# Attention's output blocks prepared in two parts and three kept on chip, and the Fourier gate columns moved from the projections into attention

## The chip, the cores and the metric

The kernel runs on one core of a Trainium2 chip. A core has TensorE (PE: matmuls; its weight loads are shown as PEld), VectorE (DVE), ScalarE (ACT), GpSimdE (POOL), and SyncE (SP), which here only issues DMA transfers. Each engine works through its own list of instructions in order, and they wait for one another through semaphores. The metric is the device time of one execution in microseconds. Less is better.

## The reference

Two layers over a latent stream of 1024 tokens and a context of 256, model width 1024. In each layer the rows are normalized and modulated (`shift` and `scale` from `c @ w_ada`), one projection to 2560 columns is split among three head groups, and one output projection joins them:

```python
px = split_cols(hx @ w_in[l])            # q 512, k 128, v 128, g_att 512, a 256, b 256, g_conv 256, f_u 256, g_four 256
attn   = windowed_attention(rope(q), rope(k), v, kc, vc, sink)  # 8 heads, 2 kv heads, 128-token blocks,
                                                                # keys: block-1, block, block+1, and all 256 of the context
y_conv = silu(layer_norm(depthwise_conv31(a * sigmoid(b))))
y_four = real(fft2(f_u)) @ w_four + b_four
y = concat([attn * silu(g_att), y_conv * silu(g_conv), y_four * silu(g_four)], -1)
x = x + gate * (y @ w_out[l])
```

The context stream goes through layer 0 in the same way (its attention is over its own keys alone); in layer 1 only its keys and values are needed. At the end comes one more normalization of the latent rows. All inputs are fp32.

## The kernel before

Every large product is made of three matmuls (`mm3`, lines 195 to 197): each operand is kept as a high part, rounded by ScalarE, and a low part, the rest, by a subtraction on Vector or GpSimd (`split`). Tokens lie in ten blocks of 128, 0 to 7 latent, 8 and 9 context. Projections go by 128 columns and chunks of 512, 512 and 256 tokens (`CHUNKS`; the context's chunk is left out in layer 1 but for keys and values). One chunk is 24 matmuls.

A layer has two stages:

**Projections.** `todo` lists the columns, `projections` makes them chunk by chunk: convolution input (`C_A`, `C_B`), then two tiles of Fourier gate columns (`C_GF`), keys, values, queries. After each chunk the loop takes one piece of side work from `side()`: the Fourier branch (`four`), the rope tables, the adaptive sums of this layer's gate (`gate_sums`) and, in layer 0, of the next layer's modulation (`ada1`: a piece with the sums of four loaded weight tiles, which starts the next four loads, then a piece that makes columns of them). It also takes convolution taps from the queue `back` (`fill_v`): 31 taps for each of two channel tiles and each token span, each one Vector instruction, up to a budget of time per chunk. The helper `Behind` puts these background instructions behind the last foreground instruction of Vector written before them.

**Attention.** `Attention.step` is one step of a software pipeline over (block, pair of heads), four to a block: scores of step i, transposes of the probabilities of step i-1, values and output of step i-2. Layer 0 has 40 steps of 10 blocks, layer 1 has 32 of 8, and each has two more that empty the pipeline. The latent blocks 1 to 6 have five key tiles of 128, 0 and 7 have four, the context blocks two. With each step goes one filler, a piece of other matmul work: first, from `rest()`, the rest of `pj` (attention gate columns `C_GATT`), with pieces of the convolution's norm `cn` once `back` is empty, then the convolution gate chunks (`C_GC`), and then the output projection in halves of 512 columns, `OP.half(i, h)`, which need block i's attention. `post` and `late` are queues of Vector work that wait for the next step's start or this step's end. Banks of the tags `mm` and `pt` (two each) hold matmul results in PSUM; fillers in attention use `mm` alone; `mmx` takes both by turns. `t512` is a small tile with four buffers.

The attention output of a block, `ot`, is stored to DRAM (`od`), and `Out.load` loads it back in the order of channels, with the other two branches' part (`yd`) and the attention gate (`sgd`). `Out.prep` gates the attention part and splits all 1024 columns, the low part on GpSimd while attention runs. In the loop, the halves of the last two blocks are left until after it.

The order of instructions on each engine is fixed when the program is built: a scheduler takes, at each simulated time, the ready instruction with the lowest priority number, and numbers rise in the order in which the code is written.

Of the kernel before, what the change touches and what calls it, by code (L numbers as in the profile page):

```python
# [16 lines left out]
ALU = mybir.AluOpType  # L17
# [4 lines left out]
P = 128  # L22
# [117 lines left out]
def tile_backbone(ctx: ExitStack, tc: tile.TileContext, a, out):  # L140
# [32 lines left out]
    def fill_v(us):  # L173
        V.background = True
        while back and us > 0:
            t, f = back.popleft()
            f()
            us -= t
        V.background = False

# [364 lines left out]
    def conv_taps(l, ct, u, z, spans):  # L545

        w = lambda j: cw[:, ct, l * KC + j:l * KC + j + 1]

        def first(s0, s1):
            V.tensor_scalar(out=z.cols(s0, s1), in0=u.cols(s0, s1), scalar1=w(15),  # L550
                            scalar2=col("conv_b", l * 2 + ct), op0=ALU.mult, op1=ALU.add)

        def tap(s0, s1, j):
            d = j - 15
            o0, o1 = max(s0, s0 - d), min(s1, s1 - d)
            V.scalar_tensor_tensor(out=z.cols(o0, o1), in0=u.cols(o0 + d, o1 + d), scalar=w(j),
                                   in1=z.cols(o0, o1), op0=ALU.mult, op1=ALU.add)
        for s0, s1 in spans:
            us = 1.25 if s0 == 0 else 0.4
            back.append((us, lambda a=(s0, s1): first(*a)))  # L560
            for j in range(KC):
                if j != 15:
                    back.append((us, lambda a=(s0, s1, j): tap(*a)))
        back.append((0.0, u.put))
# [276 lines left out]
    class Attention:  # L841
# [3 lines left out]
        def __init__(self, l, order, qd, kk, vv, od):  # L845
            self.l, self.qd, self.kk, self.vv, self.od = l, qd, kk, vv, od
            self.steps = [(b, pr) for b in order for pr in range(4)]
            self.q, self.st, self.done, self.next = {}, {}, [], 0
# [122 lines left out]
        def output(self, i):  # L971
            (b, pr), z = self.steps[i], self.st.pop(i)
            z["tmp"] = t512()[:, :256]
            r0, r1 = (slice(0, HD), slice(HD, P)) if pr < 2 else (slice(HD, P), slice(0, HD))
            S.activation(z["tmp"][r0], z["o"][r1], AF.Copy)
            ot = self.os[:, 0:512].rearrange("p (j t) -> p j t", j=4)
            r0 = slice(0, HD) if pr < 2 else slice(HD, P)
            j0 = (pr % 2) * 2
            V.tensor_tensor(out=ot[r0, j0:j0 + 2, :], in0=z["tmp"][r0].rearrange("p (h q) -> p h q", h=2),
                            in1=z["o"][r0].rearrange("p (h q) -> p h q", h=2), op=ALU.add)  # L980
            if pr == 3:
                nc.sync.dma_start(out=self.od[:, b * P:(b + 1) * P].rearrange("(j p) t -> p j t", p=P), in_=ot)
                self.os.put()
                self.done.append(b)
# [86 lines left out]
    class Out:  # L1071


        def __init__(self, l, order, wo, od, sgd, yd, x1d, xnd):
            self.l, self.order, self.wo, self.src = l, order, wo, (od, sgd, yd)
            self.x1d, self.xnd = x1d, xnd
            self.raw, self.y = {}, {}
# [3 lines left out]
        def load(self, i):  # L1081
# [6 lines left out]
            nc.sync.dma_start(out=yv[:, 0:4, :], in_=od[:, t0:t0 + P].rearrange("(k p) t -> p k t", p=P))  # L1088
# [6 lines left out]

        def prep(self, i):

            if i >= len(self.order) or i in self.y:
                return
            self.load(i)  # L1100
            (raw, yh, yl), yv, sg = self.raw[i]
            V.scalar_tensor_tensor(out=yv[:, 0:4, :], in0=yv[:, 0:4, :], scalar=0.5, in1=sg,
                                   op0=ALU.mult, op1=ALU.mult)
            split(yh, yl, raw)
            self.y[i] = yh, yl

        def half(self, i, h, bank, quick=False):
# [14 lines left out]
            for k in range(NK):  # L1122
                ks = slice(k * P, (k + 1) * P)
                mm3(o, (yh[:, ks], yl[:, ks]), (self.wo.hi[k][:, hs], self.wo.lo[k][:, hs]), k == 0, k == NK - 1)
# [156 lines left out]
    for l in range(DEPTH):  # L1281
# [39 lines left out]
        def side():  # L1321

            yield from four
            tab.extend(bufs.get("rope") for _ in range(2))
            for i, name in enumerate(("k_cos", "k_sin")):
                nc.sync.dma_start(out=tab[i].lat, in_=a[name])
# [43 lines left out]
        def gf_evac(m):  # L1370
            def f(o, c0, c1):
                drain(four)
# [27 lines left out]
        att = Attention(l, order, qd, kk, vv, od)  # L1400
# [3 lines left out]
        for m in range(2):  # L1404
            todo.append((C_GF + m * P, full) + gf_evac(m) + (mmx,))
# [6 lines left out]
        budget = [(3.0 if t[0] < C_V else 5.0) * (0.5 if c == 2 else 1.0) for t in todo for c in t[1]]  # L1412
# [4 lines left out]
        for i in range(q_at):  # L1417
            c = next(pj)
            steps(sd)
            if i >= k_at:  # L1420
                steps(kp)
# [14 lines left out]
        OP = Out(l, order, wo, od, sgd, yd, x1d, xnd)  # L1436
# [5 lines left out]
        def rest():  # L1442
# [3 lines left out]
            for i, c in enumerate(pj):  # L1446
                if i == 4 * len(full) - 2:
                    raw = w_begin(l, C_GC)
                if i == 4 * len(full) - 1:
# [46 lines left out]
        seq = deque([(0, 1), (1, 1)] + [(i, h) for i in range(2, end - 1) for h in range(2)])  # L1496
# [9 lines left out]
        while att.next < len(att.steps) + 2:  # L1506
# [5 lines left out]
            if loaded < end and loaded < len(att.done) and len(whole_ones) >= loaded - 1:  # L1512
                OP.load(loaded)
                loaded += 1
            can = seq and seq[0][0] in OP.y
            if loaded - 1 not in OP.y:
                late.append(lambda i=loaded - 1: OP.prep(i))
            att.step((lambda: next_half(mm)) if can else None)
        holding[0] = False
# [132 lines left out]
```

## Time and profile before

| | |
|---|---|
| median of 3 runs | 1202.81 us (1198.1 to 1203.62) |
| profiled execution | 1202.68 us, span of its instructions 1200.6 us |
| busy: PE, PEld | 1103.3 us (92%), 925.9 us (77%) |
| busy: DVE, ACT, POOL | 820.6 us (68%), 554.7 us (46%), 295.0 us (25%) |
| mean granted TensorE clock | 0.964 |
| DMA | 146.49 MB, mean 122 GB/s |

The span runs from the first to the last instruction of the profiled execution; what lies around it is the difference to that execution's time. The granted clock is a mean of two levels, 1.00 (2.4 GHz) and 0.50 (1.2 GHz). A matmul's end is modelled in the profile, so that successive ones overlap in it.

### The profile page before, as it was taken

What the parts mean: (1) busy time and instruction counts of PE and PEld (TensorE: products, weight loads), DVE (VectorE), ACT (ScalarE), POOL (GpSimd) and SP (SyncE); (2) the same over time, 40 slices, a digit from 0 to 9 for tenths busy, and PEclk for the clock granted to TensorE, in tenths of its full rate; (3) what the DMA queues carried; (4) which work ended last, traced back from release to release, by engine and by line L of the source; (5) the groups of instructions that cost most, each with busy time, mean ns of one, the idle gap of its engine ahead of it and who ended that gap; (6) DMA issues with size and microseconds to landing.
All of it is one profiled execution on the core that took longest, in us unless ns stands there. A gap on an engine that the chain in (4) does not pass through costs nothing.

```text
span 1200.6 us, 17131 instructions
## 1 busy us (share of the span) xinstructions
PE 1103.3 (92%) x6165; PEld 925.9 (77%) x6165; DVE 820.6 (68%) x1665; ACT 554.7 (46%) x1209; POOL 295.0 (25%) x266
## 2 busy tenths in 40 slices
PE   5799999999999989999889999999989979988866
PEld 3488887888888878888668788788778868877754
DVE  3425879999577786666755369889656786766654
ACT  5563222312566655564646652222255654545541
POOL 1212000000222443544342120000022453334321
PEclk9799999999999999999979999999989989999889
DMA  9602273744332433544436423532243453322221
GB/s 332 218 25 71 70 239 113 225 137 108 84 97 75 149 115 102 166 142 132 115 120 227 145 65 116 184 110 79 88 93 106 136 145 103 110 74 71 71 71 53
DMA packets 154093, 146.49 MB, mean 122 GB/s; under 512 B 7398, under 2 KB 131734, under 8 KB 154008
## 3 DMA queue, kind: packets, MB, share of 16 engines
q1 hardware_dynamic: 154008, 145.40, 39.5%
q8 instruction: 49, 0.80, 0.3%
q14 instruction: 36, 0.29, 0.1%
HBM read 110.49 MB, written 34.87 MB: 121 GB/s over the span
## 4 chain that ended last, share of the span: by engine, by line
PE 70%; DVE 10%; DMA 9%; ACT 4%; issue 3%; SPq 2%; POOL 1%; DVEq 0%; ACTq 0%; POOLq 0%
PE mm L195 13%; PE mm L197 13%; PE mm L196 13%; PE pt L195 5%; PE pt L196 5%; PE pt L197 5%; PE mm L963 4%; PE pt L949 4%; DMA od<-ot 3%; PE score L893 2%; DVE score L57 2%; DVE pl L57 2%; PE score L895 2%; DMA wr<-od 1%; ACT p L919 1%
## 5 line engine op out<-in xcount | busy, mean ns | idle before, releaser
L195 PE MATMUL mm<-hxh,wh 128*128 128x512 f32 (+1 forms) x808 | 311.5, 386 | 5.5 <-DVE t L57 3.2
L197 PE MATMUL mm<-hxh,wl 128*128 128x512 f32 (+1 forms) x808 | 306.7, 380 | 2.4 <-POOL wl L405 2.3
L196 PE MATMUL mm<-hxl,wh 128*128 128x512 f32 (+1 forms) x808 | 307.4, 380 | 0.0
L195 PEld LDWEIGHTS mm<-hxh,wh 128*128 128x128 f32 x808 | 153.8, 190 | 37.5 <-DVE t L57 4.3
L57 DVE SCALAR_TENSOR_TENSOR cy<-cu,cw,cy 128x1014 f32<-128x1014 f32 (+20 forms) x180 | 180.1, 1007 | 2.6
L197 PEld LDWEIGHTS mm<-hxh,wl 128*128 128x128 f32 x808 | 153.6, 190 | 30.3 <-POOL wl L405 3.1
L935 POOL TENSOR_SCALAR p<-p,st 128x640 f32<-128x640 f32 (+2 forms) x144 | 114.4, 809 | 249.1 <-DVE st L57 129.1
L196 PEld LDWEIGHTS mm<-hxl,wh 128*128 128x128 f32 x808 | 154.0, 191 | 25.0 <-issue 0.5
L405 POOL TENSOR_TENSOR wl<-wr,wh 128x1024 fp32r<-128x1024 f32 x26 | 64.2, 2468 | 396.3 <-ACT wh L404 394.1
L954 ACT ACTIVATE ph<-pt 128x512 fp32r<-128x512 f32 x184 | 97.4, 542 | 121.0 <-PE pt L949 118.2
L57 DVE TENSOR_TENSOR pl<-pt,ph 128x512 fp32r<-128x512 f32 x184 | 112.3, 616 | 57.8 <-ACT ph L954 56.4
L949 PE MATMUL pt<-ident,p 128*128 128x128 f32 x640 | 107.6, 286 | 24.5 <-DVE pl L57 19.1
L919 ACT ACTIVATE p<-score,st 128x640 f32<-128x640 f32 (+2 forms) x144 | 105.3, 734 | 36.5 <-DVE st L57 29.2
L57 DVE CUSTOM_DVE_ANT_0 score<-score,mask,nsink 128x640 f32<-128x640 f32 (+2 forms) x144 | 110.8, 782 | 13.8 <-PE score L895 13.0
L195 PE MATMUL pt<-hxh,wh 128*128 128x512 f32 (+1 forms) x296 | 112.2, 383 | 3.9 <-ACT hxh L393 2.5
L404 ACT ACTIVATE wh<-wr 128x1024 fp32r<-128x1024 f32 x56 | 59.7, 1066 | 116.5 <-PE mm L196 73.1
L196 PE MATMUL pt<-hxl,wh 128*128 128x512 f32 (+1 forms) x296 | 111.1, 376 | 0.7 <-DVE hxl L57 0.7
L197 PE MATMUL pt<-hxh,wl 128*128 128x512 f32 (+1 forms) x296 | 110.4, 373 | 0.9 <-DVE wl L57 0.9
L949 PEld LDWEIGHTS pt<-ident,p 128*128 128x128 f32 x640 | 79.8, 146 | 38.2 <-POOL p L935 8.7
L963 PE MATMUL mm<-ph,v 128*128 128x256 f32 x320 | 93.1, 314 | 13.2 <-ACT ph L954 10.7
L963 PE MATMUL mm<-pl,v 128*128 128x256 f32 x320 | 93.7, 315 | 5.3 <-DVE pl L57 4.9
L963 PEld LDWEIGHTS mm<-ph,v 128*128 128x128 f32 x320 | 64.6, 202 | 18.3 <-ACT ph L954 15.8
(220 smaller groups left out, 1797.8 us busy)
## 6 DMA issues: line engine op xcount, KB each, us to landing
wada<-w_ada SPq DMA_DIRECT2D x48, 512.0 KB, 7.0
wr<-w_in SPq DMA_DIRECT2D x38, 512.0 KB, 4.1
qq<-qd SPq DMA_DIRECT2D x36, 256.0 KB, 4.3
x1d<-x SPq DMA_DIRECT2D x10, 512.0 KB, 3.0
xnd<-xr SPq DMA_DIRECT2D x10, 512.0 KB, 3.7
p<-xnd SPq DMA_DIRECT2D x10, 512.0 KB, 4.8
sg<-sgd SPq DMA_DIRECT2D x36, 128.0 KB, 3.0
od<-ot SPq DMA_DIRECT2D x18, 256.0 KB, 2.5
```

Source lines behind the costliest of these rows:

```text
L57: r = f(*args, **kw)
L195: T.matmul(o, lhsT=lhs[0], rhs=rhs[0], start=start, stop=False)
L196: T.matmul(o, lhsT=lhs[0], rhs=rhs[1], start=False, stop=False)
L197: T.matmul(o, lhsT=lhs[1], rhs=rhs[0], start=False, stop=stop)
L404: S.activation(hi, raw, AF.Copy)
L405: (E or (G if holding[0] else V)).tensor_tensor(out=lo, in0=raw, in1=f32(hi), op=ALU.subtract)
L893: T.matmul(sc[:, c0:512], lhsT=q2[:, h, :], rhs=kx[:, k0:k0 + nl], start=fst, stop=not fst)
L919: S.activation(pp[:, j * n:(j + 1) * n], z["sc"][j][:, 768 - n:768], AF.Exp, scale=-1.0, bias=st[:, j:j + 1], accum_out=st[:, 4 + j:5 + j])
L935: G.tensor_scalar(out=pp[:, j * n:(j + 1) * n], in0=pp[:, j * n:(j + 1) * n], scalar1=st[:, 6 + j:7 + j], scalar2=1.0, op0=ALU.mult, op1=A ...
L949: T.transpose(out=bt[:, (j % 2 * 2 + y) * P:(j % 2 * 2 + y + 1) * P], in_=pp[:, c0:c0 + P], identity=ident)
L954: S.activation(ph, bt[:, :w], AF.Copy)
L963: T.matmul(o, lhsT=self.vv[kt][:, kv * P:(kv + 1) * P], rhs=y.cols(j * 256, (j + 1) * 256), start=(j == 0 and x == 0), stop=(j == z["nkt"] ...
```

## The change

Seven edits. (1) The two tiles of Fourier gate columns leave the projection stage and become the first fillers of attention; their evacuation no longer empties `four` first. (2) The rope tables are loaded at the third chunk. (3) In the last six chunks of the projections two side pieces are taken, and the taps' budgets per chunk rise from 3 and 5 us to 4 and 6. (4) Taps are given a priority number higher by 300; the context's span comes first, and its buffer is returned by itself. (5) `Out.prep` is cut in two: `prep_rest` loads and splits the 512 columns of convolution and Fourier, `prep` gates and splits the 512 of attention, with the low part on Vector; an output half takes k = 4 to 7 first and then 0 to 3. (6) In layer 1 the outputs of blocks 5, 6 and 7 (`kept`) stay in their SBUF tiles: no store, no load. (7) In layer 1 all blocks but the last are halves inside the loop, and a kept block may be loaded (its other parts) before its attention is done; `prep` is called after the step.

```diff
     def fill_v(us):
+        p0 = tc.cur_priority
+        tc.cur_priority = p0 + 300
         V.background = True
...
         V.background = False
+        tc.cur_priority = p0
...
-        for s0, s1 in spans:
+        for s0, s1 in spans[::-1]:
...
-        back.append((0.0, u.put))
+            back.append((0.0, u.put_ctx if s0 else u.put_lat))
...
             if pr == 3:
-                nc.sync.dma_start(out=self.od[:, b * P:(b + 1) * P].rearrange("(j p) t -> p j t", p=P), in_=ot)
-                self.os.put()
+                if b in self.kept:
+                    self.kept[b] = self.os
+                else:
+                    nc.sync.dma_start(out=self.od[:, b * P:(b + 1) * P].rearrange("(j p) t -> p j t", p=P), in_=ot)
+                    self.os.put()
                 self.done.append(b)
...
-            nc.sync.dma_start(out=yv[:, 0:4, :], in_=od[:, t0:t0 + P].rearrange("(k p) t -> p k t", p=P))
+            if b not in self.kept:
+                nc.sync.dma_start(out=yv[:, 0:4, :], in_=od[:, t0:t0 + P].rearrange("(k p) t -> p k t", p=P))
...
+        def prep_rest(self, i):
+
+            if i not in self.early:
+                self.early.add(i)
+                self.load(i)
+                raw, yh, yl = self.raw[i][0]
+                split(yh[:, 512:], yl[:, 512:], raw[:, 512:])
+
         def prep(self, i):
...
-            self.load(i)
+            self.prep_rest(i)
             (raw, yh, yl), yv, sg = self.raw[i]
-            V.scalar_tensor_tensor(out=yv[:, 0:4, :], in0=yv[:, 0:4, :], scalar=0.5, in1=sg,
-                                   op0=ALU.mult, op1=ALU.mult)
-            split(yh, yl, raw)
+            os = self.kept.get(self.order[i])
+            src = os[:, 0:512].rearrange("p (j t) -> p j t", j=4) if os else yv[:, 0:4, :]
+            V.scalar_tensor_tensor(out=yv[:, 0:4, :], in0=src, scalar=0.5, in1=sg, op0=ALU.mult, op1=ALU.mult)
+            if os:
+                os.put()
+            split(yh[:, :512], yl[:, :512], raw[:, :512], V)
...
-            for k in range(NK):
+            for n in range(NK):
+                k = (n + 4) % NK
...
             yield from four
-            tab.extend(bufs.get("rope") for _ in range(2))
-            for i, name in enumerate(("k_cos", "k_sin")):
-                nc.sync.dma_start(out=tab[i].lat, in_=a[name])
...
-                drain(four)
                 gate_mul(F[m], 0.5, yd[256 + m * P:256 + (m + 1) * P, :])(o, c0, c1)
...
-        att = Attention(l, order, qd, kk, vv, od)
+        att = Attention(l, order, qd, kk, vv, od, order[5:] if last else [])
...
-        for m in range(2):
-            todo.append((C_GF + m * P, full) + gf_evac(m) + (mmx,))
...
-        budget = [(3.0 if t[0] < C_V else 5.0) * (0.5 if c == 2 else 1.0) for t in todo for c in t[1]]
+        budget = [(4.0 if t[0] < C_V else 6.0) * (0.5 if c == 2 else 1.0) for t in todo for c in t[1]]
+        for m in range(2):
+            todo.append((C_GF + m * P, full) + gf_evac(m) + (mm,))
...
             c = next(pj)
+            if i == 2:
+                tab.extend(bufs.get("rope") for _ in range(2))
+                for t, name in zip(tab, ("k_cos", "k_sin")):
+                    nc.sync.dma_start(out=t.lat, in_=a[name])
             steps(sd)
+            if i >= q_at - 6:
+                steps(sd)
...
-                if i == 4 * len(full) - 2:
+                if i == 6 * len(full) - 2:
...
-        seq = deque([(0, 1), (1, 1)] + [(i, h) for i in range(2, end - 1) for h in range(2)])
+        seq = deque([(0, 1), (1, 1)] + [(i, h) for i in range(2, end if last else end - 1) for h in range(2)])
...
-            if loaded < end and loaded < len(att.done) and len(whole_ones) >= loaded - 1:
+            if loaded < (end + 1 if last else end) and (last or loaded < len(att.done)) \
+                    and len(whole_ones) >= loaded - 1 and (order[loaded] in att.done or order[loaded] in att.kept):
                 OP.load(loaded)
+                late.append(lambda i=loaded: OP.prep_rest(i))
                 loaded += 1
             can = seq and seq[0][0] in OP.y
-            if loaded - 1 not in OP.y:
-                late.append(lambda i=loaded - 1: OP.prep(i))
             att.step((lambda: next_half(mm)) if can else None)
+            if order[loaded - 1] in att.done:
+                OP.prep(loaded - 1)
```

## Rows read from the trace of the kernel before

**Rows 1.** The page: busy us by engine; a DMA group, KB each, us to landing.

```profile
PE 1103.3 (92%) x6165; PEld 925.9 (77%) x6165; DVE 820.6 (68%) x1665; ACT 554.7 (46%) x1209; POOL 295.0 (25%) x266
...
wada<-w_ada SPq DMA_DIRECT2D x48, 512.0 KB, 7.0
```

**Rows 2.** First to last tap: us; busy PE, PEld, DVE, ACT, POOL (x count); PEclk.

```profile
118.72:294.36 175.64, 175.64 (x1062) 144.64 (x1060) 157.36 (x242) 41.94 (x80) 0.00 (x0) 1.00 0.46 146
714.20:851.44 137.24, 137.24 (x706) 112.43 (x705) 123.61 (x147) 33.62 (x58) 0.00 (x0) 1.00 0.38 120
```

**Rows 3.** The same view, stretches of attention and the end (last columns: DMA share, GB/s).

```profile
476.26:566.56 90.30, 89.42 (x519) 78.54 (x518) 60.88 (x166) 50.78 (x119) 43.43 (x39) 1.00 0.44 140
566.56:629.57 63.01, 51.99 (x261) 41.81 (x260) 41.29 (x127) 34.22 (x96) 27.25 (x31) 0.87 0.39 120
1043.87:1171.94 128.07, 103.33 (x575) 88.34 (x574) 82.93 (x208) 66.00 (x157) 44.51 (x39) 0.91 0.26 72
1171.94:1200.60 28.66, 17.14 (x73) 13.19 (x72) 12.15 (x27) 3.65 (x7) 3.50 (x2) 0.93 0.16 55
399.63:461.83 62.20, 56.15 (x338) 49.41 (x337) 52.74 (x103) 37.94 (x90) 29.95 (x25) 0.97 0.41 126
962.08:993.57 31.49, 23.43 (x124) 20.72 (x125) 26.44 (x45) 17.12 (x37) 15.36 (x11) 0.89 0.48 141
```

**Rows 4.** TensorE in order of time: first scores of each layer; one filler's bounds.

```profile
302.32 0.68 PE L893 MATMUL score<-kh,q 128*128 128x256 f32 x1
...
877.45 0.38 PE L893 MATMUL score<-kh,q 128*128 128x256 f32 x1
...
906.93 0.40 PE L195 MATMUL mm<-hxh,wh 128*128 128x512 f32 x1
...
912.39 0.38 PE L949 MATMUL pt<-ident,p 128*128 128x128 f32 x2
```

**Rows 5.** TensorE by line, 476.26 to 566.56, 566.56 to 629.57, 1043.87 to 1171.94.

```profile
L195 PE MATMUL mm<-hxh,wh 128*128 128x512 f32 x80 | 31.5, 394 | 0.0
...
L895 PE MATMUL score<-kh,q 128*128 128x256 f32 x20 | 5.6, 281 | 0.0
...
L195 PE MATMUL mm<-hxh,wh 128*128 128x512 f32 x32 | 13.1, 409 | 0.7 <-ACT wh L404 0.7
...
L895 PE MATMUL score<-kh,q 128*128 128x256 f32 x20 | 7.4, 374 | 1.0 <-ACT p L919 1.0
...
L195 PE MATMUL mm<-hxh,wh 128*128 128x512 f32 x55 | 23.4, 426 | 0.0
...
L895 PE MATMUL score<-kh,q 128*128 128x256 f32 x28 | 8.0, 285 | 0.0
```

**Rows 6.** The chain that ended last, its end: start us, us, what.

```profile
1171.96 2.26 DMA od<-ot
1174.24 2.86 DMA wr<-od
1177.22 0.70 DVE wr L57
...
1181.13 0.50 PE pt L197
...
1191.18 0.24 PE mm L197
```

**Rows 7.** The tile of weights and output blocks: ns min/median/max of its instructions.

```profile
L404 ACT ACTIVATE wh<-wr x56: 1041/1061/1237, 16.9 to 1177.9; 128x1024 fp32r<-128x1024 f32 x56
...
L57 DVE TENSOR_TENSOR wl<-wr,wh x30: 1214/1220/2160, 18.0 to 1179.1; 128x1024 fp32r<-128x1024 f32 x30
```

**Rows 8.** Vector's waits, 1043.87 to 1200.6: us in total, times, longest.

```profile
DVE wr L57 <- DMA wr<-od: 8.4, 2, 5.3
```

**Rows 9.** The Fourier output and the convolution's sums: ns min/median/max of Vector's instructions.

```profile
L57 DVE SCALAR_TENSOR_TENSOR F<-F,t x10: 417/684/691, 168.0 to 781.4; 128x512 f32<-128x512 f32 x8, 128x256 f32<-128x256 f32 x2
...
L57 DVE SCALAR_TENSOR_TENSOR cy<-cu,cw,cy x180: 456/1267/1294, 119.6 to 850.2; 128x1009 f32<-128x1009 f32 x8, 128x1010 f32<-128x1010 f32 x8, 128x1011 f32<-128x1011 f32 x8, 128x1012 f32<-128x1012 f32 x8
```

More of the change, by code (lines that the diff above doesn't have):

```diff
@@ L841, in tile_backbone, with __init__ @@
     class Attention:
-        def __init__(self, l, order, qd, kk, vv, od):
+        def __init__(self, l, order, qd, kk, vv, od, kept):
             self.l, self.qd, self.kk, self.vv, self.od = l, qd, kk, vv, od
+            self.kept = {b: None for b in kept}
             self.steps = [(b, pr) for b in order for pr in range(4)]
@@ L1071, in tile_backbone, with __init__ @@
     class Out:
-        def __init__(self, l, order, wo, od, sgd, yd, x1d, xnd):
+        def __init__(self, l, order, wo, od, sgd, yd, x1d, xnd, kept):
             self.l, self.order, self.wo, self.src = l, order, wo, (od, sgd, yd)
-            self.x1d, self.xnd = x1d, xnd
-            self.raw, self.y = {}, {}
+            self.x1d, self.xnd, self.kept = x1d, xnd, kept
+            self.raw, self.y, self.early = {}, {}, set()
             self.fin = []
@@ L1121, in half @@
             o = bank()
-            for k in range(NK):
+            for n in range(NK):
+                k = (n + 4) % NK
                 ks = slice(k * P, (k + 1) * P)
-                mm3(o, (yh[:, ks], yl[:, ks]), (self.wo.hi[k][:, hs], self.wo.lo[k][:, hs]), k == 0, k == NK - 1)
+                mm3(o, (yh[:, ks], yl[:, ks]), (self.wo.hi[k][:, hs], self.wo.lo[k][:, hs]), n == 0, n == NK - 1)
             def f():
@@ L1435, in tile_backbone @@
         wo = Wout(l)
-        OP = Out(l, order, wo, od, sgd, yd, x1d, xnd)
+        OP = Out(l, order, wo, od, sgd, yd, x1d, xnd, att.kept)
         cn = conv_norm(l, y, n, rd)
@@ L1446, in rest @@
             for i, c in enumerate(pj):
-                if i == 4 * len(full) - 2:
+                if i == 6 * len(full) - 2:
                     raw = w_begin(l, C_GC)
-                if i == 4 * len(full) - 1:
+                if i == 6 * len(full) - 1:
                     box.append(w_split(raw))
```

## The prediction

> **What bounds the kernel now.** I read the page's engine line first, then the kernel cut into stretches, then the lines of each stretch, then the chain of waits at the end. TensorE is recorded as busy for 92% of the span, Vector for 68% [rows 1], so TensorE sets the pace, and the question is where it stands idle or runs at half clock. In the projection stage it never does: between the first and the last convolution tap of a layer it is busy 175.64 of 175.64 us and 137.24 of 137.24 us at a granted clock of 1.00 (2.4 GHz), with Vector at 157.36 and 123.61 us of the same stretches [rows 2]. Both engines are near full there. In attention there are two kinds of stretch. From 476.26 to 566.56 every attention step has a filler of 24 matmuls, and TensorE is dense at full clock. From 566.56 to 629.57 in layer 0, and from 1043.87 to 1171.94 in layer 1, most steps have none; TensorE is recorded busy for 82% and 81% and its mean clock is 0.87 and 0.91, which with two levels (1.2 and 2.4 GHz) means a quarter and a fifth of the time at the lower one [rows 3].
>
> Busy time understates this loss, since a small matmul is recorded longer than its turn on the engine, so I count work. A filler of 512 columns takes 912.39 - 906.93 = 5.46 us [rows 4]; one of 256 columns I estimate at half, 2.73. The dense stretch holds 80 first-of-three matmuls, 8 to a filler, so 10 fillers, and 20 context-score matmuls of the high key part, 2 to a step, so 10 steps [rows 5]. A step's own work is then (90.30 - 10 x 5.46) / 10 = 3.57 us for a block with five key tiles. I scale by key tiles: 2.86 for block 7 (four), 1.43 for a context block (two).
>
> Layer 0, 566.56 to 629.57: 10 steps and 32 / 8 = 4 fillers [rows 5]. The step order in the code makes them two steps of block 7 and eight of context: 2 x 2.86 + 8 x 1.43 + 4 x 5.46 = 39.0 us of work in 63.01; 24.0 us are free.
> Layer 1, 1043.87 to 1171.94: 28 / 2 = 14 steps and 55 / 8, about 7, fillers [rows 5]: 10 x 3.57 + 4 x 2.86 + 7 x 5.46 = 85.4 us in 128.07; 42.7 free.
> The end, 28.66 us: 73 matmuls of 5.46 / 24 = 0.2275 us are 16.6 us; 12.1 free.
> Why no fillers: an output half needs its block's attention. Stepping through the loop by hand, layer 0 uses its 14 output halves as fast as blocks finish and has 8 steps without; layer 1 has 10, the last five in a row.
>
> **The change, part by part.**
> *Fourier gate columns into attention.* Six chunks of layer 0 (four of 512 columns, two of 256) and four of layer 1 leave the projections: 4 x 5.46 + 2 x 2.73 = 27.3 and 21.8 us of TensorE work that is on the path there. They return as the first fillers, and all output halves come six or four steps later, so that steps now empty get one. Net, the gain is the free time they fill. By the same hand count layer 0 keeps 2 empty steps, both of the pipeline's drain, behind which block 8's halves are ready; I leave 5 us free, so 24.0 - 5 = 19.0 gained.
> In layer 1 the halves of blocks 2 to 5 run without a break, and steps 28 to 33 stay empty: the loop may load kept block 7 before block 6 is done, and afterwards it prepares only the block loaded last, so block 6 waits until the loop is over. An empty step now takes (128.07 - 7 x 5.46) / 14 = 6.4 us, six of them 38.4. Into them the scheduler, which takes whatever is ready, can put block 6's two halves (10.9) and the convolution and Fourier part of block 7's two (5.5) beside the steps' own 4 x 2.86: 27.8 us of work, 10.6 free. Gained: 42.7 - 10.6 = 32.1.
> *Blocks 5 to 7 of layer 1 kept on chip; preparation in two parts.* Three stores and three loads go. The last one is on the path: 2.26 + 2.86 us from the last attention output to the gating, 0.70 for that, then the roundings of all 1024 columns, and TensorE resumes in earnest at 1181.13 [rows 6]. Afterwards: 0.70, half of ScalarE's 1.06, half of Vector's 1.22 [rows 7], so 1.9 us with a little between them, then 24 matmuls instead of those of both halves whole. From the end of the last matmul (1191.4) to the span's end 9.2 us stay. Free time at the end 11.1 for 12.1: 1.0 gained; the moved halves are in the 32.1. Vector also stands 8.4 us behind two of these loads [rows 8], with the score work of the last steps queued after it; that stall is inside the 42.7 and goes with it.
> *Low half of the attention part on Vector.* 18 blocks x 0.6 = 11 us more Vector work, in a stage where it is free 29.42 of 90.30 us [rows 3]. Nothing, while that cover lasts; otherwise 11 us.
> *Taps.* Their number stays; larger budgets and the lower priority put them behind other Vector work. The stage shrinks by 27.3 us while Vector sheds only the two multiplies of six chunks, 2 x (4 x 0.684 + 2 x 0.417) = 7.1 us [rows 9]. If Vector keeps its present share of 0.896, (157.36 - 7.1) / 0.896 = 167.7 us must fit in 175.64 - 27.3 = 148.3: 19.4 us late; if it fills every gap, 1.9. The taps now end 8 us before the first scores (302.3 [rows 4]), so 0 to 11 us reach into attention. In layer 1, by the same working, 2.6 to 16 us late, with 26 us to spare (851.44 to 877.45). In attention Vector has 2.9 us a step; a tap of 1.27 us [rows 9] can stand before a score or a low half. Four such steps, one tap each: 5 us, between 0 and 11.
> *The gate as filler.* It adds one multiply and holds a small tile a step longer than the attention gate. The nearest rows are the convolution gates: 62.20 - 56.15 = 6.0 us not busy around six chunks in layer 0 and 31.49 - 23.43 = 8.1 around the last in layer 1 [rows 3]. Between 0 and 14; I take 3, because the early steps lack the output-weight work of those stretches. The ten stores on SP's queue move with them, behind multiplies that come a step later; loads queued behind them are issued a step ahead or more.
> *Adaptive sums, two pieces per chunk at the end of the stage.* A piece now follows its four loads (512 KB each, 7.0 us to land [rows 1]) by one chunk, 5.5 us and what lies beside it: up to 1.5 us for each of three, none if other chunks cover it. I take 2 of 5.
> *Rope tables earlier, context taps first, the order of k:* nothing; projection chunks cover the loads, and the sums are the same. Uncovered, a late table costs one load.
>
> **Sum.** 1202.7 (span 1200.6 plus 2.1 around it; the median is 1202.8, so no correction) - 19.0 - 32.1 - 1.0 + 5 + 3 + 2 = 1160.6. I say **1161 us**.
> The Trainium skill (Trace Analysis, Identifying the Most-Contended Engine) has TensorE judged by the busy share of weight loads rather than of matmuls. By it, with the dense stretch as full measure (78.54 / 90.30 = 0.870), the work is 41.81 / 0.870 = 48.1 and 88.34 / 0.870 = 101.6 us, and only 14.9 and 26.5 are free; the time would be 1202.7 - 9.9 - 15.9 - 1.0 + 10 = 1186. The trace bears it out in part: weight loads at the lower clock may be recorded longer, which counts idleness as work.
>
> **Rivals.**
> *Less free time than counted, 1186.* If steps of few key tiles cost more than I scale, the free time is nearer 15 and 26 us. For it: each empty step is a chain through four engines, which a filler doesn't shorten. Against: the steps between 476 and 566 have the same waits and no idleness.
> *Vector sets the projection stage, about 1190.* It keeps its 0.896 share, and TensorE stands at the convolution's mean until the taps end: 19.4 + 16 = 35 us late one for one in place of my 5, and half of the gate costs: 1202.7 - 52.1 + 35 + 5 = 1191. For: rows 2. Against: the slack of 8 and 26 us, and that the priority moves the taps alone. The Trainium skill (TensorE: Matmul & The Clock Gate, Architectural detail) calls VectorE's queue strictly first in, first out; the 8.4 us behind two loads agree, and a tap placed too early would hold the rest likewise.
> *Block 6 isn't lifted into the last steps, 1172.* The halves stay behind the loop: 10.9 more.
> *The stage doesn't shrink at all, 1200.* All 49.1 us come back as waiting for Vector: 1202.7 - 52.1 + 49.1 = 1199.7. Against: Vector's 18.3 and 13.6 idle us in rows 2.
> *Slower, 1211.* One of two matmul banks stays taken until the gate's first multiply, while the convolution's norm takes small tiles too. From 52.1 / 10 = 5.2 us per gate chunk on, this eats the gain; at 6 it is 1202.7 - 52.1 + 60 = 1211. The rows show 1 to 2 for the convolution gates.
>
> **Chances.** Forecast 0.53 (its own range 1140 to 1176), less free time 0.14, Vector 0.13, block 6 0.08, no shrinking 0.06, slower 0.06. A difference under 0.5% (6 us) can't be told from none: faster 0.87, same 0.07, slower 0.06. Low end: all idleness but the last 11 us filled and no costs gives 1202.7 - 24.0 - 42.7 - 1.0 = 1135, too good for steps whose waits remain; I put 1140. High end: 1192, which takes in the Vector case and leaves out the last two, 0.12, and some below.
>
> **What would show it.** Right: the first scores near 275 in layer 0; fillers in every step until the context blocks end; in layer 1 a mean clock near 1.00 from the first score until block 6, and no load of attention output for blocks 5 to 7; some 16 to 17 us from the last attention output to the end. Wrong: taps beside the first scores with TensorE waiting for them; idle score steps early in attention; a long wait of TensorE for weight sums before the first scores; block 6's halves after the last attention output.

## The result and the profile after

The changed kernel takes 1181.9 us (median of 4 runs, 1179.8 to 1184.7) against 1200.5 for the one before on the same chip: a ratio of 0.983, with an interval of 0.981 to 0.986. It is faster, by 18.6 us between these medians and by 20 us by the ratio, where 42 were forecast. Its profiled execution has a span of 1177.8 us against 1200.6, so 22.8 less; the ledger below is made on that.

The first line of the page after, which answers to [rows 1]:

```profile
PE 1093.8 (93%) x6165; PEld 919.9 (78%) x6165; DVE 816.3 (69%) x1678; ACT 557.2 (47%) x1227; POOL 287.1 (24%) x271
```

The windows of the kernel after. The first two are the tap stretches [rows 2]; the others answer to [rows 3]: the six convolution-gate chunks of layer 0 up to the first output half, the same kind of stretch in layer 1 (from its last convolution-gate chunk to the second output half), the end of attention in layer 0, the end of layer 1 in two pieces, and the time behind the last attention output.

```profile
core 0: us, PE busy (x) PEld busy (x) DVE busy (x) ACT busy (x) POOL busy (x), PEclk, DMA share, GB/s
114.70:273.30 158.60, 155.05 (x947) 125.32 (x947) 146.05 (x230) 38.84 (x75) 0.00 (x0) 1.00 0.50 149
705.00:828.60 123.60, 120.56 (x622) 97.04 (x620) 115.73 (x140) 30.79 (x54) 0.00 (x0) 0.99 0.37 114
427.72:497.12 69.40, 59.69 (x343) 52.94 (x341) 53.50 (x105) 38.41 (x92) 27.18 (x27) 0.90 0.44 133
976.97:1011.43 34.46, 27.59 (x124) 23.42 (x123) 26.76 (x45) 17.80 (x40) 13.95 (x10) 0.79 0.58 157
553.30:631.40 78.10, 77.30 (x414) 66.35 (x413) 48.60 (x154) 37.09 (x104) 37.88 (x41) 1.00 0.59 186
1064.10:1118.90 54.80, 53.70 (x310) 46.85 (x309) 41.74 (x99) 30.55 (x72) 21.40 (x21) 1.00 0.31 97
1118.90:1152.50 33.60, 25.72 (x155) 21.43 (x154) 21.92 (x70) 18.02 (x46) 8.39 (x10) 0.95 0.14 48
1152.50:1177.80 25.30, 16.10 (x72) 12.98 (x70) 10.86 (x28) 3.23 (x7) 2.54 (x2) 0.89 0.11 42
```

What to see. The end of layer 0, a quarter of it at the lower clock before, is now full: 77.30 of 78.10 us at 1.00. In layer 1 TensorE is busy for 53.70 of 54.80 us up to 1118.90 and then has empty steps. But the middle of attention grew: six gate chunks that took 62.20 us take 69.40, and the clock there fell from 0.97 to 0.90; in layer 1 31.49 became 34.46 and 0.89 became 0.79 (this second growth does not hold up below).

The first scores of the two layers, TensorE in order of time (two answers; [rows 4] of before):

```profile
279.25 0.68 PE L898 MATMUL score<-kh,q 128*128 128x256 f32 x1
852.60 0.38 PE L898 MATMUL score<-kh,q 128*128 128x256 f32 x1 [0.91 <-DVE q L57]
```

They cut the span in three pieces, in which the forecast's terms can be summed (the costs of taps, gate and sums shared evenly between the layers):

```
                                    before   after   change   forecast's terms
start to first scores, layer 0      302.32   279.25   -23.1   -27.3 + 1                      = -26.3
to first scores, layer 1            575.13   573.35    -1.8   +27.3 - 21.8 - 19.0 + 4 + 1    =  -8.5
to the end                          323.15   325.20    +2.1   +21.8 - 32.1 - 1.0 + 4         =  -7.3
sum                                                   -22.8                                    -42.1
```

So 3, 7 and 9 us are missing, and the experiments ask where each went. These are single executions, though. Two kernels of the experiments (e3_block6 and e10_keep_more) have the same instructions in the same order as the changed one up to the first scores of layer 1, and their first two pieces are 278.39 and 569.59, and 275.77 and 576.07. The 3 of the first piece lie within that spread of 3.5 us; the 7 of the second are as large as its spread of 6.5, and stand on the mean of the three, 573.0.

### The profile page after: what moved, and what is told of

Read it like the earlier page. It is cut to its first block, busy times and chain, and to the rows that moved or that the text cites. A ratio compares the mean times of both kernels' runs of the same rounds, so it can differ in the third digit from the quotient of the medians.

```text
span 1177.8 us, 17175 instructions
## 1 busy us (share of the span) xinstructions
PE 1093.8 (93%) x6165; PEld 919.9 (78%) x6165; DVE 816.3 (69%) x1678; ACT 557.2 (47%) x1227; POOL 287.1 (24%) x271
## 4 chain that ended last, share of the span: by engine, by line
PE 73%; DMA 10%; DVE 9%; ACT 3%; SPq 2%; issue 2%; POOL 0%; DVEq 0%; ACTq 0%; POOLq 0%
PE mm L198 13%; PE mm L199 13%; PE mm L200 13%; PE pt L198 5%; PE pt L199 5%; PE mm L968 4%; PE pt L200 4%; PE pt L954 4%; DMA wada<-w_ada 3%; PE score L898 2%; PE score L900 2%; DVE score L57 2%; DMA wr<-od 2%; DVE pl L57 1%; PE score L383 1%
## 5 line engine op out<-in xcount | busy, mean ns | idle before, releaser
L198 PE MATMUL mm<-hxh,wh 128*128 128x512 f32 (+1 forms) x832 | 319.1, 384 | 7.2 <-DVE t L57 4.4
L199 PE MATMUL mm<-hxl,wh 128*128 128x512 f32 (+1 forms) x832 | 315.0, 379 | 0.0
L200 PE MATMUL mm<-hxh,wl 128*128 128x512 f32 (+1 forms) x832 | 314.2, 378 | 0.0
L198 PEld LDWEIGHTS mm<-hxh,wh 128*128 128x128 f32 x832 | 157.9, 190 | 39.4 <-DVE t L57 5.4
L57 DVE SCALAR_TENSOR_TENSOR cy<-cu,cw,cy 128x1009 f32<-128x1009 f32 (+25 forms) x180 | 175.5, 1003 | 0.9
L57 DVE TENSOR_TENSOR pl<-pt,ph 128x512 fp32r<-128x512 f32 x184 | 111.7, 616 | 70.7 <-ACT ph L959 69.3
L408 POOL TENSOR_TENSOR wl<-wr,wh 128x512 fp32r<-128x512 f32 (+1 forms) x31 | 56.7, 1830 | 387.7 <-ACT wh L407 387.6
L407 ACT ACTIVATE wh<-wr 128x1024 fp32r<-128x1024 f32 (+1 forms) x74 | 61.7, 850 | 115.1 <-PE mm L199 78.5
L198 PE MATMUL pt<-hxh,wh 128*128 128x512 f32 (+1 forms) x272 | 103.2, 383 | 1.4 <-ACT gsum L342 1.1
L199 PE MATMUL pt<-hxl,wh 128*128 128x512 f32 (+1 forms) x272 | 101.3, 374 | 0.7 <-DVE hxl L57 0.7
L200 PE MATMUL pt<-hxh,wl 128*128 128x512 f32 (+1 forms) x272 | 100.8, 371 | 0.0
```

The costliest lines, as they stand in the source:

```text
L57: r = f(*args, **kw)
L198: T.matmul(o, lhsT=lhs[0], rhs=rhs[0], start=start, stop=False)
L199: T.matmul(o, lhsT=lhs[0], rhs=rhs[1], start=False, stop=False)
L200: T.matmul(o, lhsT=lhs[1], rhs=rhs[0], start=False, stop=stop)
L407: S.activation(hi, raw, AF.Copy)
L408: (E or (G if holding[0] else V)).tensor_tensor(out=lo, in0=raw, in1=f32(hi), op=ALU.subtract)
```

## Experiments

Times are medians; ratios are to the kernel before, run on the same chip beside them.

**Either half of the change alone.** The first (e1_fillers_only) leaves the output blocks as they were before. The second (e2_gf_back) is the changed kernel with this edit, the drain and the two index lines put back too:

```diff
+        for m in range(2):
+            todo.append((C_GF + m * P, full) + gf_evac(m) + (mmx,))
         k_at = sum(len(t[1]) for t in todo) + 3
...
-        for m in range(2):
-            todo.append((C_GF + m * P, full) + gf_evac(m) + (mm,))
```

> The kernel before with the projection-side edits alone: Fourier gate chunks as first fillers, early rope tables, two side pieces in the last six chunks, larger budgets, taps reordered and with the priority. Output blocks as before (whole preparation, nothing kept, the last two blocks' halves after the loop). Theory that the gain is free time filled by the ten moved chunks: 12 to 18 us faster than before (ratio 0.985 to 0.990), with the context blocks' steps of layer 0 dense. Rival, the gain is the output blocks' (loads that Vector stood behind, the short end): under 6 us faster (above 0.995).

> The changed kernel with the Fourier gate chunks back in the projections (with both banks' tags and the Fourier branch emptied first); everything else of the change stays. Theory of the filled free time: 3 to 8 us faster than before (0.993 to 0.998), from the end and the loads alone. Rival, the output blocks carry the gain: 12 us or more (at or under 0.990).

Measured: fillers alone 1191.7 us, 0.992 (0.989 to 0.995), between what the two theories expected. Gate back in the projections 1187.8 us, 0.989 (0.987 to 0.992): the rival's number, and the theory that the gate's move carries the change falls. By the ratios the gate's move is worth 0.006 of before (7 us) and the edits of the output blocks 0.009 (11 us). Where the gate's move is lost is looked for in the first scores with the gate put back, and the page's span:

```profile
303.46 0.68 PE L898 MATMUL score<-kh,q 128*128 128x256 f32 x1
877.69 0.39 PE L898 MATMUL score<-kh,q 128*128 128x256 f32 x1 [0.46 <-DVE q L57]
span 1186.1 us, 17137 instructions
```

Moving the gate takes 24.2 us from the first piece, where 27.3 us of work leave. It takes 0.9 from the second (574.23 to 573.35), though 5.5 us more work comes in than goes, and adds 16.8 to the third (308.4 to 325.2) for 21.8 us of work. So 6.4 and 5.0 us of idle time are filled on balance, and 3.1 us of idle time are new in the first piece: 8.3 us between these two executions, 7 by the ratios.

**Block 6 prepared in the loop (e3_block6).** The changed kernel prepares only the block that was loaded last:

```diff
-            if order[loaded - 1] in att.done:
-                OP.prep(loaded - 1)
+            for j in range(loaded):
+                if order[j] in att.done:
+                    OP.prep(j)
```

> The changed kernel, but after each step every loaded block whose attention is done is prepared, not only the one loaded last; so block 6 of layer 1 is prepared inside the loop and its halves are fillers of the last steps. Theory that the order of the loop keeps them out and the empty steps could take them: 7 to 11 us faster than the changed kernel (1171 to 1175, 0.974 to 0.978 of before). Rival, the last steps are chains that no filler shortens and the halves would merely stretch them: within 2 us of the changed kernel.

Measured: 1173.4 us, 0.976 (0.973 to 0.979), 0.0068 of before or 8.2 us under the changed kernel; the intervals are apart, and the theory was right. In the kernel after, Vector, ScalarE and TensorE in order of time show why (three answers):

```profile
1131.14 0.42 DVE L57 TENSOR_TENSOR ot<-t,mm 64x256 f32<-64x256 f32 x1
...
1132.11 0.69 DVE L57 SCALAR_TENSOR_TENSOR wr<-ot,sg 128x512 f32<-128x512 f32 x1
...
1133.60 0.89 DVE L57 TENSOR_TENSOR wl<-wr,wh 128x512 fp32r<-128x512 f32 x1
...
1132.83 0.63 ACT L407 ACTIVATE wh<-wr 128x512 fp32r<-128x512 f32 x1 [0.25 <-DVE wr L57]
...
1143.68 0.44 PE L954 MATMUL pt<-ident,p 128*128 128x128 f32 x2 [1.21 <-POOL p L940]
...
1145.81 0.39 PE L198 MATMUL mm<-hxh,wh 128*128 128x512 f32 x1
...
1151.41 0.40 PE L198 MATMUL pt<-hxh,wh 128*128 128x512 f32 x1
```

Block 6 is ready at 1134.5. Its preparation, which the code has behind the loop, was lifted into the last steps; its halves were not. The first begins at 1145.81, ahead of no more than the last seven matmuls of attention (1150.58 to 1151.29), and the second at 1151.41, behind them; TensorE waits for POOL in between. Why the scheduler lifted the one and not the other is not shown. With block 6 in the loop, the windows of the last steps and of the end:

```profile
1111.40:1151.90 40.50, 35.06 (x201) 29.83 (x199) 26.04 (x82) 18.95 (x48) 10.99 (x12) 0.96 0.15 52
1151.90:1168.30 16.40, 5.77 (x25) 4.43 (x24) 7.03 (x16) 2.07 (x5) 0.00 (x0) 0.80 0.08 32
```

From the last attention output to the end it is 16.40 us, with 25 matmuls, instead of the changed kernel's 25.30 with 72. The halves are not free in the last steps: from the first scores of layer 1 (847.98) to the last attention output it is 303.9 us, for 299.9. So 4.9 of the 9.5 us between the two profiled executions lie in the third piece; the other 4.6 lie where both programs are the same. The runs on the middle of attention, but for the last, are built on this one.

**Weight sums spread (e4_early_pieces).** The second piece of the adaptive sums goes with chunks 3 to 6 in place of the last six (`if 3 <= i < 7`), on the changed kernel.

> The changed kernel with the second side piece taken in chunks 3 to 6 in place of the last six. Theory that pieces taken in pairs meet their loads too early: TensorE's waits for the modulation weights in layer 0 and for the gate's sum row in layer 1 go (together 4 to 9 us of free time before the first scores), 4 to 8 us faster than the changed kernel (0.976 to 0.980). Rival, the loads themselves are late because the stage is shorter: the waits stay, within 2 us.

Measured: 1180.7 us, 0.981 (0.979 to 0.984): no difference from the changed kernel that can be told. The waits are there. TensorE's waits of the whole span, after (two lines), before, and in this run:

```profile
PE mm L288 <- DMA wada<-w_ada: 11.8, 12, 4.0
PE mm L361 <- DMA gsum<-b_ada: 1.9, 1, 1.9
```

```profile
PE mm L285 <- DMA wada<-w_ada: 8.5, 8, 4.0
```

```profile
PE mm L288 <- DMA wada<-w_ada: 7.8, 8, 3.7
```

The changed kernel's 3.3 us more for the modulation weights (2.0 and 1.1 in e3_block6 and e10_keep_more, whose first piece is the same program) are gone in this run, as they are with the gate put back (7.6 us, 8 times); so is the wait for the gate's sum row in layer 1. But nothing was gained: in this run TensorE waits for Vector at the first scores instead, and layer 0's convolution-gate chunks begin 153.95 us after them, with the clock lower, where the changed kernel has 148.47. First scores and that stretch, then the same stretch after:

```profile
278.10 0.47 PE L898 MATMUL score<-kh,q 128*128 128x256 f32 x1 [3.59 <-DVE q L57]
...
278.10:432.05 153.95, 148.60 (x910) 131.73 (x911) 106.34 (x232) 92.55 (x218) 40.86 (x39) 0.97 0.27 76
```

```profile
279.25:427.72 148.47, 144.02 (x910) 128.69 (x909) 103.97 (x231) 92.73 (x219) 41.40 (x39) 1.00 0.28 79
```

**The middle of attention: whose queue?** Four single edits of the kernel with block 6 in the loop. The output weights' casts on ScalarE (e7_casts_scalar):

```diff
-            split(..., self.raw[h, k], V if k % 2 else G, k % 2 == 1)
+            split(..., self.raw[h, k], V if k % 2 else G)
```

> The changed kernel with block 6 prepared in the loop (e3_block6, 0.976 of before), and the output weights' high halves rounded on ScalarE alone (8 casts a layer leave Vector, 0.4 to 1.5 us each). Theory, the idle time that the fillers should have removed came back in the middle of attention because Vector's queue is full of the output weights' splitting there (Vector 15.84 of 16.00 us busy from 475 to 491, with score masks queued behind): 4 to 8 us faster than e3_block6, ratio to before 0.970 to 0.973, and TensorE's gaps of 3 to 4 us in those two stretches halved. Rival, the chain through the four engines sets these steps: within 3 us of e3_block6.

The low half of the attention part on POOL while attention runs (`split(yh[:, :512], yl[:, :512], raw[:, :512])`, without its last argument V):

> e3_block6 with the low half of the attention part computed on POOL again while attention runs. Theory, this low half costs Vector nothing because it lies beside TensorE's fillers: within 2 us of e3_block6 (0.976 of before). Rival, it holds Vector's queue until its rounding is done (5.6 us at 980 to 985 of the changed kernel, with attention's work behind it): 3 to 8 us faster, 0.970 to 0.974. Third, the slower POOL delays the blocks: 2 to 6 us slower.

The six first loads of output weights one chunk earlier (the two lines of `wo.load()` moved ahead of `project(box[0], 0, ...)`):

> e3_block6 with the first six loads of output weights issued one convolution-gate chunk earlier. Theory, the first splits bunch because their weights land late (8 pieces between 436 and 447, after loads issued at 426 to 432 behind stores that waited 13 us for their multiplies): 3 to 6 us faster than e3_block6, ratio 0.971 to 0.974. Rival, Vector has the same work to do in the same steps: within 2 us.

Blocks 2 to 7 of layer 1 kept (`order[2:]` in place of `order[5:]`):

> e3_block6 with blocks 2 to 7 of layer 1 kept on chip instead of 5 to 7. Theory, in layer 1 Vector's 9.7 us of waiting for loads of attention output (the longest 4.0) hold score work behind them: 3 to 6 us faster than e3_block6, ratio 0.971 to 0.974. Rival, these waits lie beside TensorE's fillers: within 2 us.

Measured, against 0.976 (0.973 to 0.979): casts on ScalarE 1169.2 us, 0.972 (0.970 to 0.975); low half on POOL 1170.0, 0.972 (0.970 to 0.974); early loads 1175.5, 0.978 (0.975 to 0.981); more blocks kept 1168.5, 0.972 (0.969 to 0.974). Loading earlier gains nothing, so that theory falls. The other three each point to 5 us, but their intervals meet that of the kernel they are compared with at the edge. And none shortens the stretch in question: with the casts on ScalarE its six gate chunks run from 430.15 to 497.99, still 67.8 us; over nine kernels with the gate as filler and the pieces of the output weights where the scheduler puts them (the changed one and all others but the two run in place below) it is 66.6 to 70.7. Vector's load alone is not the cause there.

**The pieces' place.** In the trace with the casts on ScalarE, that engine waits 2.48 us for the load of a piece of output weights, with attention's rounding behind it. In the changed kernel ScalarE's queue has four such roundings (`hxh<-wor`) nearly together, two of them behind waits for their loads (ScalarE in order of time):

```profile
433.77 0.60 ACT L517 ACTIVATE t<-mm 128x512 f32<-128x512 f32 x1 [1.00 <-PE mm L200]
434.26 1.08 ACT L959 ACTIVATE ph<-pt 128x512 fp32r<-128x512 f32 x2
436.14 0.63 ACT L407 ACTIVATE hxh<-wor 128x512 fp32r<-128x512 f32 x1 [0.80 <-PE mm L200]
437.55 0.29 ACT L932 ACTIVATE st<-nsink,st 128x1 f32<-128x1 f32 x1 [0.77 <-DVE st L57]
437.75 0.62 ACT L407 ACTIVATE hxh<-wor 128x512 fp32r<-128x512 f32 x1
439.25 0.63 ACT L407 ACTIVATE hxh<-wor 128x512 fp32r<-128x512 f32 x1 [0.88 <-DMA wor<-w_out]
443.51 0.63 ACT L407 ACTIVATE hxh<-wor 128x512 fp32r<-128x512 f32 x1 [3.64 <-DMA wor<-w_out]
444.05 0.36 ACT L959 ACTIVATE ph<-pt 128x256 fp32r<-128x256 f32 x1
```

Vector's four stand beside them, and all eight of the first half run between 436 and 447. The code gives two of these pieces to each of the last four gate chunks, which begin at 455.07, 464.93, 471.27 and 481.35; the scheduler lifted all eight ahead of them. The edit ties each piece to the last instruction that the code gave the same engine ahead of it, on the kernel that keeps blocks 2 to 7 (e11_in_place); on the changed kernel alone it was not run. Three more runs go with it: the two small edits without it (e12_small_parts), all together (e13_all), and the kernel before with nothing but this edit (e14_before_in_place).

```diff
-    V, S, G, T = Behind(tc, nc.vector), nc.scalar, nc.gpsimd, nc.tensor
+    V, S, G, T = Behind(tc, nc.vector), Behind(tc, nc.scalar), Behind(tc, nc.gpsimd), nc.tensor
...
+            V.background = S.background = G.background = True
             split(self.hi[k].lat[:, hs], ...)
+            V.background = S.background = G.background = False
```

> e10_keep_more (0.9715 of before) with the pieces of the output weights' splitting held at the place that the program gives them. In e10_keep_more as in the changed kernel, all eight pieces of a half stand together in the engines' queues, ahead of attention's own work (layer 0: 8 within 10 us), although the program spreads them, two to a step in layer 0. Theory, this bunch makes the idle time in the middle of attention (by step in e10_keep_more about 20 us in layer 0 and 17 in layer 1): held in place, 8 to 20 us faster than e10_keep_more, ratio 0.955 to 0.965, with TensorE's gaps there under 1.5 us. Rival, the splitting is the same work for ScalarE, Vector and POOL wherever it stands: within 3 us. Third, the last pieces come later and delay the output halves: slower.

> e10_keep_more with the output weights' casts on ScalarE (as in e7) and the low half of the attention part on POOL (as in e8). Each of the three alone was 3 to 5 us faster than e3_block6. Theory, they take away different waits: another 5 to 8 us faster than e10_keep_more, ratio 0.965 to 0.967. Rival, they shorten the same stretch, whose end another chain sets: within 2 us of e10_keep_more.

> e12_small_parts with the pieces held in place as in e11. If the place of the pieces is the cause, 8 to 15 us faster than e12_small_parts, ratio 0.952 to 0.960; if Vector's and ScalarE's load is, within 3 us of e12_small_parts.

> The kernel before with nothing changed but the pieces of the output weights' splitting held at the place that the program gives them (as in e11, where it gave 0.0073 of before). In the kernel before, these stretches hold about 9.5 us of idle time by step in layer 0 and 15 in layer 1; in the changed kernel 19.5 and 20. Theory, the bunch costs more once the Fourier gate's fillers stand ahead of it, and this is where about half of the missing gain went: here 0 to 5 us faster, ratio 0.996 to 1.000. Rival, the bunch cost the kernel before as much, and has nothing to do with the missing gain: 8 to 12 us faster, ratio 0.990 to 0.993.

Measured: in place 1158.9 us, 0.964 (0.961 to 0.968), 0.0073 or 8.8 us under 0.9715 (0.969 to 0.974); the intervals are apart, and the theory's range held. (That range was 8 to 20 us; waits of TensorE in its stretch are 1.2 us at the longest.) The two small edits added to 0.9715 without it: 1162.6, 0.968 (0.964 to 0.972), undecided between its theories. All together: 1153.2 us, 0.960 (0.956 to 0.963), 9.9 us under the two small edits without it, as the place of the pieces as cause would have it. The kernel before, in place: 1196.7 us, 0.995 (0.993 to 0.997), 6 us, between the two theories. The windows tell more, from the first convolution-gate chunk of layer 0 to the first output half: more blocks kept, the same in place, all together, the kernel before in place, and the changed kernel with the gate put back (five answers):

```profile
424.23:494.79 70.56, 58.65 (x343) 52.24 (x341) 53.54 (x105) 38.42 (x92) 26.66 (x27) 0.93 0.44 131
```

```profile
424.07:486.44 62.37, 56.75 (x346) 50.45 (x345) 44.22 (x97) 36.20 (x90) 19.08 (x22) 0.97 0.45 138
```

```profile
429.37:491.19 61.82, 55.76 (x343) 49.87 (x342) 41.40 (x90) 37.35 (x93) 23.14 (x25) 0.97 0.47 138
```

```profile
400.16:462.38 62.22, 55.51 (x341) 49.26 (x340) 46.67 (x100) 37.04 (x90) 23.76 (x21) 0.98 0.42 125
```

```profile
407.87:468.47 60.60, 54.09 (x334) 47.34 (x332) 52.97 (x104) 37.91 (x90) 25.64 (x23) 1.00 0.43 132
```

In the kernel before this stretch takes 62.20 us [rows 3] and, in place, 62.22: there the bunch costs nothing in layer 0. With the gate put back, and all of the output blocks' edits kept, it takes 60.60: the growth belongs to the gate's move. With the gate moved the bunch costs 8.2 (70.56 to 62.37), and the clock of 0.97 comes back when it is held in place. Over the whole time the difference is small: in place gains 8.8 us in the one kernel and 6 in the other. The 6 us that the kernel before gains lie behind the first scores of layer 1 (878.05 and then 317.35 us to its end of 1195.4, for 877.45 and 323.15).

## Why the forecast was right in direction and twice too large

**What sets the time.** Right: TensorE, and the idle steps at the end of attention. The 24.0 us free in layer 0's end are gone (0.80 us not busy, clock 1.00); I had left 5. But half of that came up again ahead of the end. From the first scores to the last output matmul of layer 0's attention, before and after:

```profile
302.32:631.92 329.60, 309.63 (x1807) 269.12 (x1806) 225.77 (x563) 190.68 (x463) 132.40 (x125) 0.97 0.39 118
```

```profile
279.25:630.20 350.95, 335.56 (x1977) 295.73 (x1975) 245.07 (x593) 198.38 (x486) 129.94 (x129) 0.98 0.40 120
```

Six gate chunks and one output half more, 27.3 + 5.5 = 32.8 us of work, make it 21.4 us longer: 11.4 us of idle time were filled on balance, where 19.0 less some 4 of costs were forecast. The rival with less free time gave 1186, close to the 1181.9 measured, but not for its reason: the fillers filled the steps that they reached, and idle time came up elsewhere. (By the Trainium skill, Perfetto Trace Analysis, Identifying the Most-Contended Engine, the busy share of weight loads had given that rival's number; in layer 0's end 14.9 us were free by it and 24.0 by mine, and the trace after is full there.)

**The projection stage.** Right: first scores at 279.25, near the 275 of the forecast, and the 3 us missing there are within the spread of one program. Vector did not set it. Its share of the tap stretches rose from 0.896 to 146.05 / 158.60 = 0.921 and to 115.73 / 123.60 = 0.936, and the taps ended 6 and 24 us ahead of the first scores. The 5 us for taps in attention were not paid, and the rival of 1190 is refuted. The weight sums were put at 2 us between 0 and 5, with a long wait for them as a sign of being wrong. TensorE waits 3 to 5 us more for them in the two layers (11.8 + 1.9 for 8.5, with the spread above), but the run without these waits was no faster, so their cost in time stays open. From the end of layer 0's attention to the first scores of layer 1 it is 222.40 us for 245.53 before: 23.1 less for 27.3 us of work that left it (four gate chunks, and one output half that now runs earlier). So 4.2 us are lost there, where 1 was forecast.

**The step that failed first** is "the scheduler, which takes whatever is ready, can put block 6's two halves (10.9)" into layer 1's last steps. It did not: they ran at the loop's end and behind it. Taken into the loop they gave 8.2 us by the ratios (4.9 in the third piece of the profiled executions), so the rival that I gave 0.08 is what happened, and its 10.9 was too high: a filler in the last steps lengthens them. The rest of the missing 9 in the third piece, 1 to 4 us, stays open. The middle stretch of layer 1 (34.46 for 31.49) is no answer to it, because with block 6 in the loop the same instructions take 31.72 there, at a clock of 0.95 for 0.79:

```profile
972.75:1004.47 31.72, 24.58 (x126) 20.04 (x125) 27.10 (x49) 18.55 (x41) 13.94 (x10) 0.95 0.60 170
```

**The second** is the cost of 3 for the gate as filler, with no term for what stands behind it. I read the convolution-gate stretches of [rows 3] as a price per gate, and carried them over as if the gate chunks were all that changed there. The stretch that grew, 62.20 us to 69.40, has none of the moved chunks in it; what bunches in it is the output weights' splitting. Those 7.2 us are not by themselves the 7 missing in the second piece: that sum is 3.6 in layer 0's attention, where the end gave 4.2 more than forecast and the rest lost it again, and 3.1 in layer 1's projection stage. That the bunch is what costs the stretch its time, the runs in place show for the line with more blocks kept; why it costs the kernel before nothing in layer 0, they don't.

**Low half on Vector, at nothing.** Vector's cover was read from the dense stretch, 29.42 us free of 90.30 [rows 3], but the blocks 0 and 1 are prepared in the middle stretch. There Vector waits in line (Vector's groups by line, 980 to 1000, two lines, and ScalarE's rounding from its order of time):

```profile
L57 DVE TENSOR_TENSOR wl<-wr,wh 128x512 fp32r<-128x512 f32 x1 | 1.4, 1369 | 5.6 <-ACT wh L407 5.6
...
L57 DVE SCALAR_TENSOR_TENSOR wr<-wr,sg 128x512 f32<-128x512 f32 x1 | 0.7, 691 | 0.9 <-DMA wr<-od 0.9
...
984.42 1.15 ACT L407 ACTIVATE wh<-wr 128x512 fp32r<-128x512 f32 x2 [5.11 <-PE mm L199]
```

The subtraction stands 5.6 us at the head of Vector's queue until ScalarE has rounded, and ScalarE's rounding itself stands 5.1 us until a matmul of TensorE is done; attention's work is behind both. (That agrees with the Trainium skill, TensorE: Matmul & The Clock Gate, Architectural detail, which has VectorE's queue strictly in order.) POOL in its place gave about 5 us, which its interval doesn't settle.

**The end.** Right in its parts: gating 0.69 us right behind the last attention output, then the halved rounding and subtraction (three lines of Vector's order of time):

```profile
1152.08 0.42 DVE L57 TENSOR_TENSOR ot<-t,mm 64x256 f32<-64x256 f32 x1 [5.23 <-ACT t L980]
1152.54 0.69 DVE L57 SCALAR_TENSOR_TENSOR wr<-ot,sg 128x512 f32<-128x512 f32 x1
1153.93 0.69 DVE L57 TENSOR_TENSOR wl<-wr,wh 128x512 fp32r<-128x512 f32 x1 [0.70 <-ACT wh L407]
```

That is 2.1 us from the last output's end to the last operand, for 1.9 forecast. With block 6 out of the way the end is 16.40 us (e3_block6), for "some 16 to 17".

**The priority of the taps** was to put them behind other Vector work, and moves nothing: without it the program has the same instructions in the same order on all five engines.

## What to carry to other kernels

Idle time can be filled only by work that the program lets into it. Count, step by step, which instructions the code gives to a step and whether its scheduler really lifts what is ready; here it lifted block 6's preparation but not its halves, and pulled weight preparation forward into a bunch. And when fillers are put ahead of a chain, look at what they push together further on: the stretch that grows need not be the one that was edited. And before a few missing microseconds of one piece are explained, see how far that piece moves between executions of the same program; here it was 3 to 6.

## What the runs showed of the hardware that was not expected

In the kernel after, a weight cast of 128x512 on Vector takes 0.41 us at 995.12, where POOL does nothing, and 1.51 at 969.30, where POOL subtracts from 968.82 to 973.62; so pieces in a bunch can cost more than the same pieces apart. (Over layer 0's pieces the median cast is 0.92 us in the changed kernel and 0.42 in place; in the kernel before, bunched too, it is 0.43, and there the median subtraction is 1.02 for 0.68.) Beside POOL's scaling of the probabilities (995.78 to 998.57) the cast at 997.58 takes 0.41 all the same. The Trainium skill (SBUF — State Buffer, SBUF: two separate sides) has Vector and GpSimd share one pair of ports under an exclusive lock: of certain Vector operations and GpSimd's, the one that starts first holds it to its end and the other waits. The subtraction agrees with that, the scaling does not show it.

And the clock did not follow the sum of the gaps: in layer 0's middle stretch it was 0.97 with 6.1 us not busy (before), 0.90 with 9.7 (after), and 0.93 with 11.9 (more blocks kept).
